# Other places in memory for some weight pieces of a two-layer hybrid network: a second pair in each branch, a cycle of four pairs in one FFN

## The chip, the core and the metric

The kernel runs on one core of a Trainium2 chip. The metric is device time in microseconds of one execution. TensorE (PE in the profile, PEld for its weight loads), VectorE (DVE), ScalarE (ACT), GpSimd (POOL) and SyncE (SP, which issues most DMAs here) run from queues of their own.

## The reference

One sequence of 256 tokens, width 1024, goes through two layers. Each layer has three sub-layers, so there are six branches, which the kernel numbers s = 0 to 5: FFN, hybrid mixer (RG-LRU and SSD), FFN, FFN, mLSTM, FFN. Each branch is normed and modulated by a projection of `c`, and added back through a gate:

```python
def swiglu(h, w_gate, w_up, w_down):
    return (jax.nn.silu(h @ w_gate) * (h @ w_up)) @ w_down
...
h = modulate(x, 0)
x = x + HALF_STEP * (1.0 + mod[:, 0, 2]) * swiglu(h, ffn_w_gate[layer, 0], ffn_w_up[layer, 0], ffn_w_down[layer, 0])
h = modulate(x, 1)
y = hybrid_mixer(h, ...) if layer % 2 == 0 else mlstm_block(h, ...)
x = x + (1.0 + mod[:, 1, 2]) * y
```

D_FF is 2816. All is float32, and every matrix is used once.

## The kernel before, in words

**Weights as a stream.** The host lays all large weight matrices out as 2928 tiles of 128 x 128 in the order of their use, and groups eight of them to a piece: 366 pieces of 128 x 1024 float32, 512 KB each. `Weights._piece` brings one in: a DMA on SP's queue (L90) into one of three `wraw` buffers, a cast on ScalarE to the high part `whi` (L102, fp32r), and a subtraction on VectorE for the low part `wlo` = raw - high (L103). Both parts have six buffers, and a piece is prepared up to four ahead of its use. Between the pieces, `ada_block` (L213 to L220) streams 144 rows of the modulation matrix through the same queue and reduces them on VectorE.

**Matmuls.** The activations stand in memory as high and low parts too, in `hb` (the normed input), `ph` (the FFN's middle) and others. A narrow tile takes three matmuls of 256 columns: high weights with high and with low activations, low weights with high ones (`multiply`, L334 to L336). In the down projections of FFNs and mLSTM a wide tile takes two: high weights with both parts at once, 512 columns (L439), and low weights with 256 (L441). Each matmul loads its 128 x 128 weights first. A narrow piece is thus 24 matmuls, a wide one 16.

**Branches in pieces.** The branches begin at pieces 0, 66, 120, 186, 252 and 300. In an FFN the first 44 pieces (gate and up) are narrow and the last 22 (down) wide; the hybrid branch has 54 narrow pieces; mLSTM has 32 narrow ones and 16 wide. In the last branch the final two pieces count as narrow. I call the branches FFN 0, hybrid, FFN 2, FFN 3, mLSTM and FFN 5. Every branch starts with the norm, whose chain runs through VectorE and ScalarE (`begin`), beside matmuls of 258 columns.

**Places.** Tile pools are laid out one behind the other in each partition. The distance of a part from the start of `hb` is the sum of what lies between: `hb` itself 24576 bytes, a pad of 112 floats (`xpad`, L174), `rs` and two `ssq` tiles of 1024 bytes, three `wraw` of 4096, then six `whi` of 4096 and six `wlo` of 4608. So `whi` begins 24576 + 448 + 3072 + 12288 = 40384 bytes behind `hb`, which is 448 more than a multiple of 512, and the `wlo` tiles likewise. All tiles of a piece lie 512 bytes apart, and all chunks of `hb` 1536, so the remainder by 512 is one number for each part of a piece; I call it the part's place. The high part stands at 448. The low part stands in its tile at an offset of 16 floats, 64 more for odd pieces, 16 more for narrow ones (L93), which gives place 64 (even) or 320 (odd) in narrow pieces and 0 or 256 in wide ones. The moving operands, `ph` and the mLSTM's `yb` among them, stand at place 0.

Of the kernel before, what the change touches and what calls it, by code (L numbers as in the profile page):

```python
# [11 lines left out]
F32 = mybir.dt.float32  # L12
F32R = mybir.dt.float32r
# [6 lines left out]
P = 128  # L20
# [32 lines left out]
SUB_TILES = [FFN_TILES, HYB_TILES, FFN_TILES, FFN_TILES, ML_TILES, FFN_TILES]  # L53
NTILE = sum(SUB_TILES)
PIECE = 8

WIDE = []
for _i, _n in enumerate((ND * NF, 0, ND * NF, ND * NF, ND * 16, ND * NF)):
    _e = sum(SUB_TILES[:_i + 1])
    WIDE.append(((_e - _n) // PIECE, _e // PIECE))  # L60
WIDE[-1] = (WIDE[-1][0], WIDE[-1][1] - 2)
LO_ROW = 384


# [6 lines left out]
class Weights:  # L71
# [14 lines left out]
    def _piece(self, i):  # L86
        nc = self.nc
        w = PIECE * P
        raw = self.raw_pool.tile([P, w], F32, tag="wraw", name=f"wraw{i}")
        nc.sync.dma_start(raw, self.src[i])  # L90


        o = 16 + 64 * (i % 2) + (0 if any(p <= i < q for p, q in WIDE) else 16)  # L93
        hi = self.part_pool.tile([P, w], F32R, tag="whi", name=f"whi{i}")
        lo = self.part_pool.tile([P, w + 128], F32R, tag="wlo", name=f"wlo{i}")[:, o:o + w]
        with self.tc.high_priority(offset=self.ahead):
            if i < 2:
                raw_hi = nc.scalar.copy(hi, raw)
                if i == 1:
                    self.tc.add_manual_dep(raw_hi.ins, self.first[1].ins.name, NOSYNC, reason="the first input first")  # L100
            else:
                raw_hi = nc.scalar.copy(hi, raw)  # L102
            self.last = nc.vector.tensor_tensor(out=lo, in0=raw, in1=hi.bitcast(F32), op=ALU.subtract)  # L103
        if i < 2:
            self.tc.add_manual_dep(self.last.ins, self.first[0].ins.name, NOSYNC, reason="the first input first")
        self.parts[i] = (hi, lo)
        self.splits[i] = (raw_hi, self.last)
        for n, ins in self.after.pop(i, ()):
            self._behind(i, n, ins)
# [25 lines left out]
def body(ctx: ExitStack, tc: tile.TileContext, a, out, dbg=None):  # L135
    nc = tc.nc
# [3 lines left out]
    xp = ctx.enter_context(tc.tile_pool(name="xp", bufs=1))  # L140
# [3 lines left out]
    modp = ctx.enter_context(tc.tile_pool(name="modp", bufs=5))  # L144
    small = ctx.enter_context(tc.tile_pool(name="small", bufs=4))
    tmp = ctx.enter_context(tc.tile_pool(name="tmp", bufs=2))
    ps_mm = ctx.enter_context(tc.tile_pool(name="ps_mm", bufs=4, space=PS))
    ps_ax = ctx.enter_context(tc.tile_pool(name="ps_ax", bufs=1, space=PS))

# [21 lines left out]


    hb = xp.tile([P, ND, 2 * LO_ROW], F32R, name="hb")
    xp.tile([P, 112], F32, name="xpad")  # L174
    hh, hl = hb[:, :, 0:T + 2], hb[:, :, LO_ROW:LO_ROW + T + 2]
    h = [hb[:, k, 0:2 * LO_ROW].rearrange("p (i t) -> p i t", i=2)[:, :, 0:T] for k in range(ND)]
    hx = [(hh[:, k, :], hl[:, k, :]) for k in range(ND)]
# [16 lines left out]
    for b in range(2):  # L194
        q = fpool.tile([P, D], F32, name=f"xsq{b}")
# [893 lines left out]
    w = small.tile([P, 2], F32, tag="rs_w", name="rsw_fin")  # L1089
# [121 lines left out]
```

## Time and profile before

| | |
|---|---|
| median of 3 runs | 1138.76 us (1142.5, 1138.76, 1137.49) |
| the profiled execution's own time | 1143.54 us |
| its span | 1141.8 us |
| TensorE busy | 1116.2 us, 98% of the span |
| weight loads busy | 1064.0 us, 93% |
| VectorE busy | 957.6 us, 84% |
| ScalarE busy | 642.6 us, 56% |
| mean DMA rate | 238 GB/s |

The span is the time from the first to the last profiled instruction. Matmuls overlap in the pipeline, so an engine that is busy all the time can still be working at different paces; the distance between the starts of two matmuls says which. A window's count of instructions includes the two or three that began just before it.

### The profile page before, as it was taken

To read this page: it belongs to the slowest core of one execution; us is meant where nothing else is said; L and a number is where in the kernel's file an instruction comes from. 1 tells how busy PE (TensorE), PEld (TensorE's weight loads), DVE (VectorE), ACT (ScalarE), POOL (GpSimd) and SP (SyncE) were. 2 spreads that over 40 slices of the span, in tenths; PEclk is the share of its full clock that TensorE was granted. 3 is DMA by queue.
4 is the path that set the end of the run, shared out by engine and by line. 5 is a ranking of instruction groups with operands and counts; after the bars stand their busy time and mean duration, and the time that the engine had idled before them with its cause. 6 is when DMAs were issued, how large, how long until landed. Compare 5 with 4: busy or idle time off the path is not lost.

```text
span 1141.8 us, 21905 instructions
## 1 busy us (share of the span) xinstructions
PE 1116.2 (98%) x8548; PEld 1064.0 (93%) x8548; DVE 957.6 (84%) x1831; ACT 642.6 (56%) x1074; POOL 8.7 (1%) x25
## 2 busy tenths in 40 slices
PE   7999999999999999999999998999999999999997
PEld 6999988999988999999899998889999989999987
DVE  7989999999879798788889888989879988766562
ACT  4464444788976554444454454457765556544552
POOL 0000000000000000000000000000000000000000
PEclk8999999999999999999999999999999999999999
DMA  8989989656555658888848899983432364875551
GB/s 332 343 306 360 378 308 323 207 181 193 198 167 170 197 201 316 311 296 306 286 150 291 306 349 328 329 296 109 160 120 93 112 223 149 273 240 201 188 200 41
DMA packets 75273, 272.25 MB, mean 238 GB/s; under 512 B 8449, under 2 KB 9121, under 8 KB 75170
## 3 DMA queue, kind: packets, MB, share of 16 engines
q1 hardware_dynamic: 74160, 268.99, 67.2%
q0 software_dynamic: 432, 1.10, 0.4%
q8 instruction: 67, 1.10, 0.4%
q10 hardware_dynamic: 578, 0.76, 0.2%
q14 instruction: 36, 0.29, 0.1%
HBM read 269.77 MB, written 1.05 MB: 237 GB/s over the span
## 4 chain that ended last, share of the span: by engine, by line
PE 73%; DVE 14%; DMA 6%; ACT 4%; issue 3%; ACTq 0%; SPq 0%
PE od L439 15%; PE gu L335 9%; PE gu L334 9%; PE gu L336 9%; PE od L441 8%; DVE wlo L103 5%; DMA wraw<-in_wst_dram 5%; DVE ada L220 3%; ACT whi L102 2%; DVE hb L351 1%; DMA wgr<-in_ml_wg_dram 1%; PE od L334 1%; PE up L335 1%; PE up L336 1%; DVE ht L348 1%
## 5 line engine op out<-in xcount | busy, mean ns | idle before, releaser
L102 ACT CAST whi<-wraw 128x1024 fp32r<-128x1024 f32 x364 | 380.7, 1049 | 281.3 <-DMA wraw<-in_wst_dram 154.6
L103 DVE TENSOR_TENSOR wlo<-wraw,whi 128x1024 fp32r<-128x1024 f32 x366 | 447.1, 1223 | 94.8 <-ACT whi L102 90.4
L335 PE MATMUL gu<-hb,whi 128*128 128x256 f32 x1312 | 365.8, 280 | 0.1
L336 PE MATMUL gu<-hb,wlo 128*128 128x256 f32 x1312 | 363.0, 278 | 0.0
L334 PE MATMUL gu<-hb,whi 128*128 128x256 f32 x1312 | 360.2, 279 | 1.6 <-ACT hb L350 1.5
L334 PEld LDWEIGHTS gu<-hb,whi 128*128 128x128 f32 x1312 | 245.1, 189 | 2.3 <-ACT hb L350 2.1
L335 PEld LDWEIGHTS gu<-hb,whi 128*128 128x128 f32 x1312 | 246.8, 188 | 0.3 <-DVE hb L351 0.3
L336 PEld LDWEIGHTS gu<-hb,wlo 128*128 128x128 f32 x1312 | 247.1, 188 | 0.0
L439 PE MATMUL od<-ph,whi 128*128 128x512 f32 x682 | 233.9, 391 | 5.7 <-DVE ph L328 5.7
L441 PE MATMUL od<-ph,wlo 128*128 128x256 f32 x682 | 188.9, 277 | 0.0
L220 DVE SCALAR_TENSOR_TENSOR ada<-ada,cact 128x1024 f32<-128x1024 f32 x144 | 175.1, 1219 | 0.0
L439 PEld LDWEIGHTS od<-ph,whi 128*128 128x128 f32 x682 | 128.7, 189 | 33.1 <-DVE ph L328 6.5
L441 PEld LDWEIGHTS od<-ph,wlo 128*128 128x128 f32 x682 | 128.7, 189 | 0.0
L327 ACT CAST ph<-fg 128x256 fp32r<-128x256 f32 x88 | 35.2, 406 | 91.0 <-DVE fg L470 90.6
L446 DVE SCALAR_TENSOR_TENSOR x<-od,gate,x 128x256 f32<-128x256 f32 x87 | 41.6, 482 | 23.0 <-PE od L441 11.9
L328 DVE TENSOR_TENSOR ph<-fg,ph 128x256 fp32r<-128x256 f32 x88 | 36.7, 422 | 12.9 <-ACT ph L327 12.8
L439 PE MATMUL od<-yb,whi 128*128 128x512 f32 x128 | 45.2, 397 | 0.0
L334 PE MATMUL zz<-hb,whi 128*128 128x256 f32 x128 | 37.2, 290 | 0.0
L469 ACT ACTIVATE fg<-gu 128x256 f32<-128x256 f32 x82 | 30.5, 377 | 11.6 <-PE gu L336 11.6
L336 PE MATMUL zz<-hb,wlo 128*128 128x256 f32 x128 | 36.9, 288 | 0.0
L335 PE MATMUL zz<-hb,whi 128*128 128x256 f32 x128 | 36.8, 288 | 0.0
L350 ACT ACTIVATE hb<-ht,shift 128x256 fp32r<-128x256 f32 x48 | 22.6, 505 | 24.2 <-DVE ht L348 24.2
(407 smaller groups left out, 1902.1 us busy)
## 6 DMA issues: line engine op xcount, KB each, us to landing
wraw<-in_wst_dram SPq DMA_DIRECT2D x366, 512.0 KB, 4.3
ada<-in_adaT_dram SPq DMA_DIRECT2D x144, 512.0 KB, 5.4
xn<-in_x_dram SPq DMA_DIRECT2D x2, 512.0 KB, 4.0
wgr<-in_ml_wg_dram POOLq DMA_DIRECT2D x3, 256.0 KB, 5.4
out_dram<-res ACTq DMA_DIRECT2D x2, 128.0 KB, 2.3
out_dram<-res SPq DMA_DIRECT2D x2, 128.0 KB, 2.1
out_dram<-res SPq DMA_DIRECT2D x1, 256.0 KB, 2.5
out_dram<-res ACTq DMA_DIRECT2D x1, 256.0 KB, 2.6
```

Source lines behind the costliest of these rows:

```text
L102: raw_hi = nc.scalar.copy(hi, raw)
L103: self.last = nc.vector.tensor_tensor(out=lo, in0=raw, in1=hi.bitcast(F32), op=ALU.subtract)
L220: nc.vector.scalar_tensor_tensor(out=raw, in0=raw, scalar=1.0, in1=cact, op0=ALU.mult, op1=ALU.mult, accum_out=mods[s][:, m:m + 1])
L327: nc.scalar.copy(hi, src)
L328: nc.vector.tensor_tensor(out=both[:, 1, :], in0=src, in1=hi.bitcast(F32), op=ALU.subtract)
L334: m = nc.tensor.matmul(dst, wh, both[:, 0, :], start=start, stop=False, skip_group_check=True)
L335: nc.tensor.matmul(dst, wh, both[:, 1, :], start=False, stop=False, skip_group_check=True)
L336: nc.tensor.matmul(dst, wl, both[:, 0, :], start=False, stop=stop, skip_group_check=True)
L439: nc.tensor.matmul(bank, wh, both.rearrange("p i t -> p (i t)"), start=(k == 0), stop=False, skip_group_check=True)
L441: nc.tensor.matmul(sums[0], wl, both[:, 0, :], start=False, stop=(k == len(rhs) - 1), skip_group_check=True)
L446: nc.vector.scalar_tensor_tensor(out=xs_t[d], in0=part, scalar=g[:, d:d + 1], in1=xs_t[d], op0=ALU.mult, op1=ALU.add)
L469: nc.scalar.activation(g, b[:, 0:T], AF.Silu)
```

## The change

It gives each piece a pair of places (high, low), written out in a list `PLACES`, where before only the low part's place was set. The `whi` tiles get the same slack of 128 floats as the `wlo` tiles, so that both can be moved. The default pairs stay what they were: (448, 64) and (448, 320) in narrow pieces, (448, 0) and (448, 256) in wide ones. Others get new ones:
- narrow pieces whose number in the branch leaves 6 on division by 11 (6, 17, 28, 39, 50) in all branches but FFN 2: (128, 0)
- wide pieces 1 and 8 of each wide part: (128, 192)
- the 44 narrow pieces of FFN 2: a cycle of (448, 320), (64, 448), (448, 64), (320, 192).

To make room, the pad behind `hb` shrinks from 112 to 16 floats, the scratch for software DMA descriptors at the start of memory from 8192 to 4096 bytes, and a pad of 96 floats ahead of the temporaries brings the pools behind it back to their remainders by 512. With the smaller pad both kinds of tiles begin at place 64, which is why 64 is taken off. The raw pieces, the modulation rows and the small per-column tiles begin 128 bytes further on in a block of 512.

```diff
--- before.py
+++ after.py
@@ -59,6 +59,17 @@
     _e = sum(SUB_TILES[:_i + 1])
     WIDE.append(((_e - _n) // PIECE, _e // PIECE))
 WIDE[-1] = (WIDE[-1][0], WIDE[-1][1] - 2)
+PLACES = []
+for _i in range(NTILE // PIECE):
+    _s = max(s for s in range(6) if sum(SUB_TILES[:s]) // PIECE <= _i)
+    _n = _i - sum(SUB_TILES[:_s]) // PIECE
+    _w = [_i - p for p, q in WIDE if p <= _i < q]
+    if _w:
+        PLACES.append((128, 192) if _w[0] in (1, 8) else (448, 256 * (_i % 2)))
+    elif _s == 2:
+        PLACES.append(((448, 320), (64, 448), (448, 64), (320, 192))[_i % 4])
+    else:
+        PLACES.append((128, 0) if _n % 11 == 6 else (448, 64 + 256 * (_i % 2)))
 LO_ROW = 384
 
 
@@ -90,9 +101,9 @@
         nc.sync.dma_start(raw, self.src[i])
 
 
-        o = 16 + 64 * (i % 2) + (0 if any(p <= i < q for p, q in WIDE) else 16)
-        hi = self.part_pool.tile([P, w], F32R, tag="whi", name=f"whi{i}")
-        lo = self.part_pool.tile([P, w + 128], F32R, tag="wlo", name=f"wlo{i}")[:, o:o + w]
+        oh, ol = ((n - 64) % 512 // 4 for n in PLACES[i])
+        hi = self.part_pool.tile([P, w + 128], F32R, tag="whi", name=f"whi{i}")[:, oh:oh + w]
+        lo = self.part_pool.tile([P, w + 128], F32R, tag="wlo", name=f"wlo{i}")[:, ol:ol + w]
         with self.tc.high_priority(offset=self.ahead):
             if i < 2:
                 raw_hi = nc.scalar.copy(hi, raw)
@@ -144,6 +155,7 @@
     modp = ctx.enter_context(tc.tile_pool(name="modp", bufs=5))
     small = ctx.enter_context(tc.tile_pool(name="small", bufs=4))
     tmp = ctx.enter_context(tc.tile_pool(name="tmp", bufs=2))
+    tmp.tile([P, 96], F32, name="tpad", bufs=1)
     ps_mm = ctx.enter_context(tc.tile_pool(name="ps_mm", bufs=4, space=PS))
     ps_ax = ctx.enter_context(tc.tile_pool(name="ps_ax", bufs=1, space=PS))
 
@@ -171,7 +183,7 @@
 
 
     hb = xp.tile([P, ND, 2 * LO_ROW], F32R, name="hb")
-    xp.tile([P, 112], F32, name="xpad")
+    xp.tile([P, 16], F32, name="xpad")
     hh, hl = hb[:, :, 0:T + 2], hb[:, :, LO_ROW:LO_ROW + T + 2]
     h = [hb[:, k, 0:2 * LO_ROW].rearrange("p (i t) -> p i t", i=2)[:, :, 0:T] for k in range(ND)]
     hx = [(hh[:, k, :], hl[:, k, :]) for k in range(ND)]
@@ -1200,7 +1212,7 @@
     from concourse.bass_utils import run_bass_kernel_spmd
 
     arrays = layouts(inputs)
-    nc = bacc.Bacc("TRN2", target_bir_lowering=False, num_devices=1, dynamic_dma_scratch_size=8192)
+    nc = bacc.Bacc("TRN2", target_bir_lowering=False, num_devices=1, dynamic_dma_scratch_size=4096)
     args = {n: nc.dram_tensor(f"in_{n}_dram", v.shape, mybir.dt.from_np(v.dtype), kind="ExternalInput").ap()
             for n, v in arrays.items()}
     out = nc.dram_tensor("out_0_dram", (T, D), F32, kind="ExternalOutput").ap()
```

## Rows read from the trace of the kernel before

**Rows 1.** The page: the group of instructions that makes the low parts.
```profile
L103 DVE TENSOR_TENSOR wlo<-wraw,whi 128x1024 fp32r<-128x1024 f32 x366 | 447.1, 1223 | 94.8 <-ACT whi L102 90.4
```

**Rows 2.** Busy by stretch: PE, PEld, DVE, ACT, POOL (count); clock, DMA share, GB/s.
```profile
61.50:141.40 79.90, 79.90 (x675) 79.90 (x674) 73.88 (x118) 40.71 (x63) 0.00 (x0) 1.00 0.94 351
279.90:296.90 17.00, 17.00 (x145) 17.00 (x144) 16.32 (x29) 14.83 (x29) 0.00 (x0) 1.00 0.70 230
412.20:521.10 108.90, 108.90 (x919) 108.90 (x918) 89.64 (x131) 54.12 (x81) 0.00 (x0) 1.00 0.85 300
593.80:702.60 108.80, 108.80 (x962) 108.80 (x961) 96.97 (x160) 52.80 (x79) 1.08 (x2) 1.00 0.86 304
964.30:1073.10 108.80, 108.80 (x962) 108.80 (x961) 77.64 (x112) 57.66 (x87) 0.00 (x0) 1.00 0.66 223
```

**Rows 3.** Timeline of PE, narrow: piece 127 to 164, then piece 191 to 230, first matmuls.
```profile
415.51 0.28 PE L334 MATMUL gu<-hb,whi 128*128 128x256 f32 x1
...
521.08 0.40 PE L439 MATMUL od<-ph,whi 128*128 128x512 f32 x1
...
596.54 0.28 PE L334 MATMUL gu<-hb,whi 128*128 128x256 f32 x1
...
702.62 0.39 PE L439 MATMUL od<-ph,whi 128*128 128x512 f32 x1
```

**Rows 4.** Timeline of PE, wide: piece 166 to 185, then piece 289 to 299, first matmuls.
```profile
526.55 0.39 PE L439 MATMUL od<-ph,whi 128*128 128x512 f32 x1
...
578.23 0.39 PE L439 MATMUL od<-ph,whi 128*128 128x512 f32 x1
...
920.67 0.40 PE L439 MATMUL od<-yb,whi 128*128 128x512 f32 x1
...
948.67 0.40 PE L439 MATMUL od<-yb,whi 128*128 128x512 f32 x1
```

**Rows 5.** Timeline of PE first wide piece of FFN 0 (44) and the next.
```profile
141.38 0.39 PE L439 MATMUL od<-ph,whi 128*128 128x512 f32 x1
...
144.11 0.39 PE L439 MATMUL od<-ph,whi 128*128 128x512 f32 x1
```

**Rows 6.** Timeline of PE around a wait of FFN 0.
```profile
55.47 1.07 PE L334 MATMUL gu<-hb,whi 128*128 128x256 f32 x5
56.37 0.28 PE L335 MATMUL gu<-hb,whi 128*128 128x256 f32 x1
...
56.97 0.28 PE L335 MATMUL gu<-hb,whi 128*128 128x256 f32 x1
```

**Rows 7.** The chain that ended last, shares: FFN 2 narrow, mLSTM wide.
```profile
by line: PE gu L335 34.1%; PE gu L334 33.2%; PE gu L336 32.8%
...
by line: PE od L439 64.2%; PE od L441 32.2%; PE hT L1024 3.3%; PE zz L334 0.3%; PE zz L336 0.3%; PE zz L335 0.3%
```

**Rows 8.** The chain, in order of time: end of FFN 0, hybrid branch.
```profile
193.95 0.49 DVE x L446
...
209.12 5.58 DMA wraw<-in_wst_dram
...
258.90 4.33 DMA wraw<-in_wst_dram
```

**Rows 9.** The chain, in order of time: a row of FFN 3.
```profile
605.43 5.28 DMA wraw<-in_wst_dram
```

**Rows 10.** Waits (us, times, longest): 141 to 196, 521 to 581, 596 to 720 us.
```profile
DVE x L446 <- PE od L441: 1.4, 2, 1.2
...
ACT whi L102 <- PE od L439: 24.7, 18, 1.7
...
PE od L439 <- DVE ph L328: 5.7, 2, 3.3
```

**Rows 11.** Timeline of FFN 0: the split of piece 54, its first matmul.
```profile
164.95 1.22 DVE L103 TENSOR_TENSOR wlo<-wraw,whi 128x1024 fp32r<-128x1024 f32 x1
...
168.59 0.39 PE L439 MATMUL od<-ph,whi 128*128 128x512 f32 x1
```

## What I expect, written before the run

> **What bounds the kernel now.** Read first the busy times by stretch [rows 2]. [...] So there are two paces, and the clock is not what tells them apart. The timeline gives them exactly [rows 3]: pieces 127 to 163 of FFN 2 are 37 x 24 = 888 matmuls of 256 columns in 521.08 - 415.51 = 105.57 us, 118.9 ns each; pieces 191 to 229 of FFN 3 are 936 in 106.08 us, 113.3 ns each. Shapes, places in memory and engines are the same. A wide tile (512 and 256 columns) has two paces too [rows 4]: 51.68 us / 152 = 340.0 ns in FFN 2, 28.00 us / 80 = 350.0 ns in the mLSTM branch. I call them the quick and the slow pace. The slow one costs 24 x 5.55 ns = 0.133 us a narrow piece and 8 x 10 ns = 0.080 us a wide one.
>
> Next, where the pace changes. In FFN 0 PE waits between 55.47 and 56.37 us (five matmuls that take 0.90 us instead of 0.57), and from there to 56.97 us five starts lie 120 ns apart [rows 6]; the whole rest of the narrow part stays slow (675 in 79.9 us, [rows 2]). At 141.38 us the shape changes to wide, and the first wide piece takes 144.11 - 141.38 = 2.73 us, the quick 8 x 340 ns but for 0.01 [rows 5]. So a pace, once taken, holds for tens of microseconds; a wait can turn it to slow, and another pattern of reads, without any wait, has turned it back.
>
> Then the chain that ended last, for where a slow pace counts at all. In FFN 2 it is matmuls alone, and in the wide part of the mLSTM branch 96% matmuls of its two lines [rows 7]: a nanosecond there is a nanosecond of the end. Behind FFN 0 the chain goes over to VectorE at 193.95 us and through the transfer of raw weights at 209.12 and 258.90 us [rows 8]. In FFN 3 it runs over transfers and splits, as in the row at 605.43 us [rows 9], and PE idles there once for 5.7 us behind the last ph [rows 10]. In those places PE's pace is covered.
>
> **The change part by part.** No instruction, transfer or wait is added, taken away or moved: 63 of 366 pieces get their high and low parts at another distance from the moving operand, and the pools around them shift. What is priced is therefore the pace alone.
>
> Narrow pieces with number 6, 17, 28, 39 (and 50) of each branch but FFN 2 now stand at (128, 0), in all 20; wide pieces 1 and 8 at (128, 192), in all 10. I take them as resets: for one piece (24 or 16 matmuls) the two streams of reads that PE makes meet at other places, and the pace is taken anew. No row shows these pairs. Below, a reset does nothing to the pace and costs nothing; above, it turns a slow stretch quick. I take the second, since the only change of pattern without a wait that the rows show did that [rows 5]. The FFN 2 cycle moves 33 of its 44 narrow pieces, two of every four with the high part at another place; by the same reading it never stays slow.
>
> What that gives, in the profiled execution:
> - FFN 2: the 37 slow pieces, 37 x 0.133 = 4.9 us. Nothing else is near: VectorE is busy 89.6 of 108.9 us [rows 2], and in the wide part behind it ScalarE waits 24.7 us for PE to free a buffer [rows 10], so the splits can catch up what they lose. Late next is FFN 3's norm, which starts that much earlier too. I take 4.9.
> - FFN 0: the reset at piece 17 frees pieces 18 to 43, 26 x 0.133 = 3.5 us, but not all of it arrives. VectorE is busy 73.9 of 79.9 us [rows 2], and the split of piece 54 ends at 166.17 us, 2.4 us ahead of its first matmul at 168.59 [rows 11]: no more than 2.4 can pass there. VectorE itself waits for PE only 1.4 us before the seam [rows 10], and the chain goes on through VectorE [rows 8]. So between 0 and 2.4; I take 1.4.
> - Hybrid: the same slow pace (145 starts in 17.0 us, [rows 2], as against about 152 at the quick one). The resets at pieces 83 and 116 would free about 14 pieces, 1.9 us, half of it behind ScalarE and transfers [rows 8]: 0.9, between 0 and 1.9.
> - mLSTM wide: pieces 286 to 299 behind the reset at 285, 14 x 0.080 = 1.1 us on the chain [rows 7].
> - FFN 3 narrow: quick already, and PE has 5.7 us of idle time there [rows 10]: 0 either way.
> Sum 8.3 us.
>
> Against it stands what a reset costs where the stream was quick. Priced from below at nothing and from above at the slow pace: four narrow ones of FFN 5 and five wide ones on the chain (two each in FFN 2 and FFN 5, one behind FFN 3's wait), 4 x 0.133 + 5 x 0.080 = 0.9 us; those of FFN 0 and FFN 3's narrow part lie under the covers named above. I take 0.5.
>
> The raw weights and the streamed modulation rows now begin 128 bytes further in a block of 512. All 366 splits read from the old place, 1223 ns each [rows 1], so no row shows the other. A split slower or faster by 1% would be 12 ns a piece, under VectorE's 19 us of idle time in FFN 2 [rows 2]; only FFN 0's margin would feel it, 66 x 12 ns = 0.8 us. I take 0. The smaller descriptor scratch serves only the eight transfers that GpSimd issues, most of them for FFN 3; I price it at 0, and if one came late, PE's 5.7 us of idle time in FFN 3 [rows 10] would grow by as much.
>
> Sum: 8.3 - 0.5 = 7.8 us, bounds 10.3 (all of FFN 0 and hybrid, no cost) and 4.0 (FFN 2's 4.9 alone, less 0.9).
>
> The profiled execution took 1143.54 us, 4.8 above the median of 1138.76. From its own time the sum gives 1143.54 - 7.8 = 1135.7. If the timed runs hold the same slow stretches and the difference is the profiler's, the median falls to 1131.0. The timed runs themselves spread over 5.0 us, which is what FFN 2's stretch alone is worth, so I think some of them had it quick; but nothing proves it. I forecast 1133, between the two, 0.5% below the median, which is the edge of what I call a change: 0.5% is 5.7 us, so faster means below 1133.1 and slower above 1144.5.
>
> [...]
>
> **The rivals.**
> - The place doesn't decide. The pace would then be taken at the waits [rows 6] and kept through every reset. For it: both paces occur at the same pairs [rows 3]. Against it: the turn at 141.38 us without a wait [rows 5]. Time: that of before, 1138.8, with its spread of 1137.5 to 1142.5. Chance 0.13.
> - Half works: the resets do, the FFN 2 cycle does not (it keeps default pairs in two of four pieces, so it may be slow in those), or the other way round. Without FFN 2's 4.9 us there are left 2.9 us: 1138.8 - 2.9 = 1135.9; with the cycle alone and the other parts at their cost, 4.9 - 0.9 = 4.0: 1134.8 from the median, up to 1139.5 from the profiled time. About 1137. Chance 0.13.
> - The resets throw quick stretches into the slow pace (the other side). Then FFN 5 from piece 307 on loses 37 x 0.133 = 4.9 us, and the wide parts of FFN 2 (20 pieces), FFN 3 behind the wait (14) and FFN 5 (19) lose 53 x 0.080 = 4.2 us; FFN 3's narrow part stays covered. With FFN 2 no better, 1138.8 + 9.1 = 1147.9. It is slower by my bound from 5.7 us of these on, that is FFN 5's narrow part and ten wide pieces, if FFN 2's gain is gone too; with that gain it is 1143. Against it: a new pattern led to the quick pace [rows 5]. Chance 0.12, three quarters of it slower.
>
> **How the numbers follow.** My forecast has 0.62: between 1128.5 (10.3 below the median) and 1136.5, with a little over half of it below 1133.1. That makes 0.35 faster, and 0.27 within 0.5%; "half works" adds 0.02 to faster and 0.11 to same, "place doesn't decide" 0.13 to same, "resets harm" 0.03 to same and 0.09 to slower. Faster 0.37, same 0.54, slower 0.09; since the hybrid and mLSTM branches have many short slow spells (as in [rows 2]) that I counted only in part, I move 0.04 from same to faster. The range leaves out the harm above 1141 and the lowest tail: 1129 to 1141.
>
> **What would show it.** FFN 2 at about 940 to 960 starts in 108.8 us instead of 919; FFN 0 behind piece 17 at 113.3 ns; wide tiles of the mLSTM branch at 340 ns from piece 286 on; reset pieces themselves of at most 2.85 us. The chain of FFN 0's end starts on VectorE earlier than 193.95 us by 1 to 2. The forecast is wrong if FFN 2 stays at 118.9, if FFN 3 or FFN 5 fall to it behind a reset, or if PE begins to wait for splits in FFN 0 by more than it gained.

## The result and the profile after

The changed kernel takes 1136.97 us (median of 20 runs, 1129.76 to 1143.28) where the kernel before takes 1142.09 beside it (20 runs, 1136.58 to 1148.23): a ratio of 0.9948, 95% interval 0.9928 to 0.9968. That is 0.52% less, just past the 0.5% that I called a change (the interval reaches to both sides of it), and 4 us above my forecast of 1133. Of the three runs of before that I had seen (median 1138.76), two lay at the lower end of its spread. The profiled execution took 1137.13 us as against 1143.54.

Busy by stretch after, in the columns of [rows 2]: FFN 0 from piece 18 to 43, FFN 2 from piece 127 to 163, FFN 5 from piece 306 on.

```profile
67.90:138.90 71.00, 71.00 (x627) 71.00 (x626) 67.44 (x110) 36.40 (x55) 0.00 (x0) 1.00 0.96 357
411.20:511.90 100.70, 100.70 (x891) 100.70 (x890) 83.39 (x121) 49.66 (x74) 0.00 (x0) 1.00 0.87 313
962.80:1047.80 85.00, 85.00 (x750) 85.00 (x749) 60.60 (x84) 43.29 (x66) 0.00 (x0) 1.00 0.69 236
```

FFN 2's 37 pieces, 888 matmuls, now take 100.7 us, 113.4 ns each; before it was 105.57 [rows 3]. FFN 0's 26 pieces, 624 matmuls in 71.0 us, stand at the quick pace but for the two reset pieces among them. FFN 5 is quick as before; its row holds 750 starts with three reset pieces in it, and 752 or 753 in the kernels below that have none there.

Timeline of PE after: first matmul of the reset piece 17 and of piece 18, then of the wide pieces 289 and 299 of the mLSTM branch.

```profile
65.16 0.28 PE L346 MATMUL gu<-hb,whi 128*128 128x256 f32 x1
...
68.00 0.28 PE L346 MATMUL gu<-hb,whi 128*128 128x256 f32 x1
...
914.49 0.39 PE L451 MATMUL od<-yb,whi 128*128 128x512 f32 x1
...
941.74 0.39 PE L451 MATMUL od<-yb,whi 128*128 128x512 f32 x1
```

The reset piece takes 2.84 us, 0.12 more than a quick one and within 0.02 of a piece at the slow pace (24 x 118.9 ns = 2.85 us). The wide pieces take 27.25 us, 340.6 ns a tile, as against 28.00 us before [rows 4].

By branch, from the timeline's first matmul of each (us). For each matmul that reads a weight piece, the distance to the next start is compared with the quick pace: "pace" adds up the excesses under 20 ns, "waits" those of 20 ns or more.

| branch | length before, after | difference | pace before, after | waits before, after |
|---|---|---|---|---|
| before piece 0 | 14.6, 15.4 | +0.9 | | |
| FFN 0 | 187.0, 183.8 | -3.2 | 4.4, 1.2 | 2.7, 2.8 |
| hybrid | 188.7, 187.1 | -1.6 | 5.2, 4.3 | 12.7, 11.8 |
| FFN 2 | 191.0, 186.0 | -5.1 | 5.8, 0.8 | 1.2, 1.3 |
| FFN 3 | 189.4, 192.0 | +2.6 | 0.6, 1.5 | 8.1, 9.8 |
| mLSTM | 181.1, 180.5 | -0.7 | 3.0, 1.9 | 10.6, 11.1 |
| FFN 5 to the end | 190.0, 190.6 | +0.6 | 0.7, 1.3 | 0.3, 0.3 |

Each entry is rounded by itself; unrounded, the differences add up to -6.4 us, that of the two spans (1141.8 and 1135.4). At FFN 0's end the chain that ended last, which left the matmuls only at 193.95 us before [rows 8], now runs over splits and transfers long ahead of it:

```profile
152.41 6.22 DMA wraw<-in_wst_dram
...
161.07 6.26 DMA wraw<-in_wst_dram
...
194.05 5.82 DMA wraw<-in_wst_dram
```

FFN 3 gave 2.6 back. Its rows after, where piece 232 waits for the last ph, in the columns of [rows 2]; then the two of before that answer to the last two (piece 232 begins at 699.64 after and at 708.06 before); then the wait that answers to [rows 10]:

```profile
700.00:704.00 4.00, 1.34 (x9) 0.95 (x8) 3.27 (x6) 2.67 (x5) 0.00 (x0) 0.97 1.01 368
704.00:708.00 4.00, 0.90 (x3) 0.39 (x3) 4.00 (x7) 2.25 (x4) 0.00 (x0) 0.50 0.89 280
708.00:712.00 4.00, 4.00 (x13) 3.42 (x14) 2.65 (x4) 1.29 (x2) 0.00 (x0) 0.50 0.95 349
712.00:716.00 4.00, 4.00 (x19) 3.45 (x19) 3.82 (x6) 0.94 (x2) 0.00 (x0) 0.75 0.95 365
```

```profile
716.40:720.40 4.00, 4.00 (x17) 3.45 (x17) 2.77 (x4) 1.67 (x2) 0.00 (x0) 0.66 0.97 369
720.40:724.40 4.00, 4.00 (x25) 3.53 (x25) 3.47 (x6) 0.93 (x3) 0.00 (x0) 1.00 1.01 394
```

```profile
PE od L451 <- DVE ph L340: 5.8, 2, 3.1
```

The wait itself is as long as before (5.8 us, 5.7 in [rows 10]). What grew is what follows it: PE idles, the granted clock falls to 0.50, and it stays low longer than before (a mean of 0.50 and then 0.75 in the last two rows, 0.66 and 1.00 before), and 4 us hold 13 and then 19 matmuls where they held 17 and 25. The DMA share is 0.89 or more throughout, and of the chain from 585 to 730 us 32.1% is transfers of raw weights, its costliest line: the branch is bound by its weights, as [rows 9] said.

### The profile page after: what moved, and what is told of

It is laid out like the page before. It is cut to its first block, busy times and chain, and to the rows that moved or that the text cites. A ratio compares the mean times of both kernels' runs of the same rounds, so it can differ in the third digit from the quotient of the medians.

```text
span 1135.4 us, 21905 instructions
## 1 busy us (share of the span) xinstructions
PE 1109.3 (98%) x8548; PEld 1057.5 (93%) x8548; DVE 955.4 (84%) x1831; ACT 642.0 (57%) x1074; POOL 8.8 (1%) x25
## 4 chain that ended last, share of the span: by engine, by line
PE 61%; DVE 18%; DMA 13%; ACT 5%; issue 3%; ACTq 0%; SPq 0%; DVEq 0%
PE od L451 12%; DMA wraw<-in_wst_dram 11%; DVE wlo L114 7%; PE gu L346 7%; PE gu L347 7%; PE gu L348 7%; PE od L453 6%; DVE ada L232 3%; ACT whi L113 3%; DVE hb L363 1%; DMA wgr<-in_ml_wg_dram 1%; DVE ht L360 1%; PE od L346 1%; PE up L347 1%; PE up L348 1%
## 5 line engine op out<-in xcount | busy, mean ns | idle before, releaser
L114 DVE TENSOR_TENSOR wlo<-wraw,whi 128x1024 fp32r<-128x1024 f32 x366 | 446.1, 1221 | 97.1 <-ACT whi L113 95.1
L458 DVE SCALAR_TENSOR_TENSOR x<-od,gate,x 128x256 f32<-128x256 f32 x87 | 41.5, 480 | 20.1 <-PE od L348 9.7
L453 PE MATMUL od<-yb,wlo 128*128 128x256 f32 x128 | 35.5, 279 | 0.0
```

The source lines that it names most:

```text
L453: nc.tensor.matmul(sums[0], wl, both[:, 0, :], start=False, stop=(k == len(rhs) - 1), skip_group_check=True)
L458: nc.vector.scalar_tensor_tensor(out=xs_t[d], in0=part, scalar=g[:, d:d + 1], in1=xs_t[d], op0=ALU.mult, op1=ALU.add)
```

## The experiments

All are edits of the list of pairs in the changed kernel; shifted pools, slack and scratch stay. Ratios are to the kernel before, run beside each. In the fences "85 us" is a stretch of a narrow part from its ninth piece (FFN 2: 128) or seventh (FFN 3: 192, FFN 5: 306): at the quick pace it holds 750 starts and the two or three that began before it, at the slow one 715 and those.

**Default pairs everywhere.**

```diff
-        PLACES.append((128, 192) if _w[0] in (1, 8) else (448, 256 * (_i % 2)))
-    elif _s == 2:
-        PLACES.append(((448, 320), (64, 448), (448, 64), (320, 192))[_i % 4])
+        PLACES.append((448, 256 * (_i % 2)))
     else:
-        PLACES.append((128, 0) if _n % 11 == 6 else (448, 64 + 256 * (_i % 2)))
+        PLACES.append((448, 64 + 256 * (_i % 2)))
```

> Every piece at the default pair of the kernel before; only the pools are shifted (raw weights and modulation rows 128 bytes further in a block of 512, smaller descriptor scratch, slack in the high parts). If the places decide the pace (theory), FFN 2's narrow part and the end of the mLSTM branch can run slow as before (118.9 and 350 ns) and the time is that of the kernel before: ratio 0.998 to 1.002. If the shifted pools or the chance of a wait gave the gain (rival), the ratio is that of the changed kernel, 0.995, with FFN 2 at 113.3 ns.

Ratio 0.9995 (0.9974 to 1.0017). Busy by stretch: FFN 0 from piece 18, FFN 2.

```profile
67.30:132.30 65.00, 65.00 (x576) 65.00 (x575) 61.36 (x98) 33.50 (x51) 0.00 (x0) 1.00 0.97 355
414.60:499.60 85.00, 85.00 (x718) 85.00 (x717) 69.29 (x101) 41.63 (x62) 0.00 (x0) 1.00 0.90 312
```

FFN 2 is slow again, so the shifted pools are not what made it quick. But FFN 0 is quick without any reset: at the default pairs both paces occur, and which one comes is not settled by the pairs.

**The cycle alone, and the resets alone.** Each is the changed kernel with the other edit taken back to the default pairs.

> The cycle of four pairs in FFN 2 alone, every other piece at its default pair. Theory: FFN 2's 37 slow pieces become quick, 4.9 us less than the kernel before (ratio 0.9957), and FFN 0, the hybrid and the mLSTM branch keep their slow stretches. Rival (places do not matter): ratio 1.000 and FFN 2 slow or quick by chance. If the resets were only a cost, this is the faster version: 0.993 or less.

> The resets alone, FFN 2's narrow part at the default pairs. Theory: FFN 2 slow again if a slow stretch starts there (loses 4.9 us of the changed kernel's gain), the others as in the changed kernel: ratio 0.998 to 1.001, since the gain of FFN 0 and the hybrid branch (about 4 us) was spent in FFN 3 and FFN 5 (3.1 us). If the resets carry the gain, 0.995.

Cycle alone: 0.9972 (0.9944 to 1.0000), median 1137.35. Resets alone: 0.9986 (0.9959 to 1.0014), median 1140.71. Busy by stretch, the cycle alone: FFN 2, then FFN 3 from piece 212 to 228.

```profile
413.70:498.70 85.00, 85.00 (x752) 85.00 (x751) 71.58 (x106) 43.27 (x65) 0.00 (x0) 1.00 0.91 320
644.40:692.40 48.00, 48.00 (x406) 48.00 (x405) 42.97 (x69) 22.87 (x34) 0.00 (x0) 1.00 0.93 338
```

FFN 2 is quick with the cycle. FFN 3, at default pairs, turned slow at a gap of 0.1 us in piece 211 and stayed so to the end of its narrow part, 406 starts in 48 us (quick would be 424 and the two or three before); behind the wait at piece 232 the wide pieces 234 to 251 were slow as well. Yet this branch, 191.6 us, was no longer than in the changed kernel (192.0), since the wait at piece 232 fell to 5.3 us with what follows it, from 7.7: pace in FFN 3 is covered, as two kernels below show more plainly.

Busy by stretch, the resets alone: FFN 2, then the hybrid branch from piece 89 on.

```profile
415.60:500.60 85.00, 85.00 (x752) 85.00 (x751) 69.99 (x104) 42.43 (x63) 0.00 (x0) 1.00 0.89 312
277.40:291.40 14.00, 14.00 (x121) 14.00 (x120) 12.96 (x24) 11.98 (x24) 0.00 (x0) 1.00 0.71 232
```

Here FFN 2 came out quick at its default pairs; I had expected it slow. And the hybrid branch stays slow from piece 78 to 97, right through the reset pieces 83 and 94, and again from 104 to 111 around 105 (121 starts where the quick pace gives 126, below). Of these only 94 is a plain test: gaps of 0.5 and 0.4 us lie at the end of 83, and a wait of 1.3 us right behind 105, and a pace can turn slow at a wait, as FFN 0's did at 55.47 us in before [rows 6].

Other narrow resets stood in slow stretches with no wait behind them, and there the quick pace followed at once. Behind piece 280 of the mLSTM branch, pieces 281 and 282: before, changed kernel, resets alone. Then piece 270: the resets alone, with the reset at 269, and the default pairs everywhere.

```profile
895.40:900.80 5.40, 5.40 (x47) 5.40 (x47) 4.41 (x13) 3.31 (x5) 0.00 (x0) 1.00 0.79 261
889.15:894.55 5.40, 5.40 (x50) 5.40 (x49) 4.39 (x13) 2.94 (x5) 0.00 (x0) 1.00 0.86 273
888.15:893.55 5.40, 5.40 (x50) 5.40 (x49) 4.54 (x13) 3.06 (x5) 0.00 (x0) 1.00 0.83 247
...
840.70:843.40 2.70, 2.70 (x27) 2.70 (x25) 2.27 (x9) 1.33 (x2) 0.00 (x0) 1.00 0.52 184
845.30:848.00 2.70, 2.70 (x25) 2.70 (x24) 2.28 (x8) 1.33 (x2) 0.00 (x0) 1.00 0.51 171
```

The same holds behind piece 116 of the hybrid branch, in both kernels with resets.

**One pair for a whole part.** These tell whether a pair has a pace of its own.

```diff
+        PLACES.append({0: (64, 448), 2: (128, 0), 3: (448, 320), 5: (320, 192)}[_s])
```

(in the four FFNs; the wide pieces of FFN 0 and mLSTM at (128, 192)), and

```diff
+        PLACES.append({0: (448, 64), 2: (448, 0), 3: (480, 352), 5: (384, 64)}[_s])
```

> One pair for a whole narrow part: (64, 448) in FFN 0, (128, 0) in FFN 2, (448, 320) in FFN 3, (320, 192) in FFN 5; the wide pieces of FFN 0 and mLSTM all at (128, 192). If the pace belongs to the pair, FFN 2 runs at 118.2 ns throughout (44 pieces at 0.116 us, 5.1 us more than quick), the wide parts of FFN 0 and mLSTM at 346 ns (0.050 us a piece), and the other three narrow parts at 113.3 ns whenever no wait has turned them. If it is the change of pair that costs, only the first piece of each part is slow.

> One pair for a whole narrow part: (448, 64) in FFN 0, (448, 0) in FFN 2, (480, 352) in FFN 3, (384, 64) in FFN 5. The pairs that ran quick have both parts at 64 beyond a multiple of 128, the pair (128, 0) has both at a multiple of 128. If the remainder of the high part by 128 decides, FFN 5 (384) is slow in two of three matmuls (about 116.5 ns) and FFN 2 in one of three (about 115 ns); FFN 0 at 113.3; FFN 3 in between. If only the pace at the last wait counts, each part is at 113.3 or 118.9 throughout, whatever its pair.

Busy by stretch, first kernel: FFN 0 from piece 18, FFN 2, FFN 5, then 30 us of mLSTM's wide part from piece 288.

```profile
67.10:132.10 65.00, 65.00 (x576) 65.00 (x575) 61.81 (x98) 34.71 (x54) 0.00 (x0) 1.00 0.96 356
415.50:500.50 85.00, 85.00 (x721) 85.00 (x720) 68.83 (x101) 41.35 (x62) 0.00 (x0) 1.00 0.89 310
966.40:1051.40 85.00, 85.00 (x753) 85.00 (x752) 60.91 (x85) 43.73 (x67) 0.00 (x0) 1.00 0.72 236
914.70:944.70 30.00, 30.00 (x175) 26.47 (x174) 25.45 (x39) 18.76 (x27) 0.00 (x0) 1.00 0.77 241
```

Second kernel: FFN 0, FFN 2, FFN 3, FFN 5.

```profile
68.20:133.20 65.00, 65.00 (x549) 65.00 (x548) 62.46 (x99) 34.78 (x53) 0.00 (x0) 1.00 0.97 360
423.30:508.30 85.00, 85.00 (x724) 85.00 (x723) 70.25 (x102) 41.55 (x63) 0.00 (x0) 1.00 0.90 314
605.10:690.10 85.00, 85.00 (x717) 85.00 (x716) 75.50 (x121) 39.59 (x59) 1.07 (x2) 1.00 0.89 313
974.50:1059.50 85.00, 85.00 (x724) 85.00 (x723) 59.06 (x82) 41.52 (x64) 0.00 (x0) 1.00 0.70 230
```

In these parts the pace goes with the pair. The reset pair (128, 0) is slow by itself: 721 starts, 85 / 718.5 = 118.3 ns, in all 37 pieces from 127 on with no wait among them. So are (448, 0) and (384, 64) (117.8 ns) and (480, 352) (119.0 ns). (64, 448) and (320, 192) ran quick (576 starts in 65 us, 753 in 85 us), and so did (448, 320) in FFN 3 (752 in 85 us). The default place (448, 64), held without alternating, was slow in FFN 0 (549 starts in 65 us) from a wait in piece 14 on, as the default pairs were in before, and quick in pieces 2 to 13. The wide reset pair is slow by itself too: 175 starts where the changed kernel has 179 in the same 30 us. My split by thirds (only the matmuls with the moved part slow) did not hold: (448, 0) and (384, 64) came out alike. Each of these two kernels was run once, in 1140.15 and 1152.51 us.

The second kernel also shows that pace in FFN 3 is covered. There this branch ran at the slow pace from its fifth piece to its end and took 188.5 us; with every piece at the reset pairs (next) it took 188.6. In the twelve other kernels it took 188.4 to 192.0. In the two slow ones its waits shrink to 0.3 and 1.2 us (6.3 to 9.8 in the others), and in the second kernel the clock does not fall, over 10 us from piece 232 on (the changed kernel's mean clock over the same 10 us is 0.71).

```profile
719.15:729.15 10.00, 10.00 (x59) 8.77 (x58) 8.10 (x13) 4.36 (x7) 0.00 (x0) 1.00 0.96 344
```

**Every piece at the reset pairs**, which makes the suspected cost large: (128, 0) in all narrow pieces, (128, 192) in all wide ones.

> Every narrow piece at (128, 0), every wide one at (128, 192): nothing changes from piece to piece. If these pairs are slow by themselves, FFN 2 and FFN 5 lose 5.1 us each against quick, their wide parts and mLSTM's 2.8 us, FFN 0 up to 5: 13 to 18 us above the changed kernel, ratio to before 1.006 to 1.012. If only a change of pair costs, the time is that of the changed kernel or less: 0.993 to 0.996.

Ratio 1.0104 (1.0057 to 1.0151), median 1154.05 beside 1142.98. FFN 5 has 721 starts in the 85 us and FFN 2 the same:

```profile
972.90:1057.90 85.00, 85.00 (x721) 85.00 (x720) 58.88 (x82) 41.48 (x63) 0.00 (x0) 1.00 0.70 229
```

Place alone, with the same instructions, moves this kernel by 11 us in this direction.

**The cycle in all narrow parts**, without the (128, 0) pieces.

> The cycle of four pairs in the narrow parts of all branches, no (128, 0) piece; the wide pieces as in the changed kernel. Theory: every narrow part runs at 113.3 ns, so the hybrid branch loses its two slow stretches that the (128, 0) pieces did not end (about 2 us less) and FFN 5 its four pieces of 0.116 us (0.5 us): 1 to 2.5 us below the changed kernel, ratio to before 0.9925 to 0.994. If the cycle holds the quick pace only where it was quick anyway, the ratio is 0.995 to 1.000 and slow stretches appear in FFN 0 or in the hybrid branch.

Ratio 0.9955 (0.9934 to 0.9975). The pace did what was expected: its excess over quick is 7.5 us in the whole execution (10.9 in the changed kernel, 19.7 in before), and outside the branches' starts no slow stretch of a narrow part is longer than 30 matmuls (a piece has 24). The time did not follow. The hybrid branch took 190.3 us, longer than before (188.7). Busy by stretch around its piece 112, changed kernel first, then this one:

```profile
363.00:368.00 5.00, 4.37 (x35) 3.96 (x34) 4.35 (x10) 1.66 (x3) 0.00 (x0) 1.00 0.72 233
368.00:373.00 5.00, 4.28 (x36) 3.99 (x35) 3.76 (x7) 2.97 (x5) 0.00 (x0) 1.00 0.64 233
```

```profile
363.00:368.00 5.00, 2.23 (x20) 2.04 (x18) 2.86 (x6) 0.78 (x1) 0.00 (x0) 0.94 0.81 237
368.00:373.00 5.00, 4.37 (x19) 4.20 (x20) 3.86 (x8) 2.14 (x5) 0.00 (x0) 0.50 0.36 124
```

and there, in this kernel (its lines stand two lower), the wait and then the chain:

```profile
PE od L344 <- ACT ylb L337: 3.4, 1, 3.4
```

```profile
360.97 6.15 DMA wraw<-in_wst_dram
367.22 1.04 ACT whi L111
368.27 0.31 ACT ylb L337
```

PE reaches the projection sooner, waits 3.4 us (1.3 in the changed kernel) for ScalarE's ylb, which stands in its queue behind a cast whose raw weights land after 6.15 us (4.30 in the changed kernel), and the granted clock falls to 0.50 behind the wait. In this execution the quicker pace is spent there, and more than it.

**A cycle for the wide pieces too**, by analogy: (448, 256), (64, 384), (448, 0), (320, 128).

> The cycle of four pairs in all narrow parts and a cycle of (448, 256), (64, 384), (448, 0), (320, 128) in all wide parts; no (128, 0) and no (128, 192). If the slow stretches go where the pair of places changes from piece to piece among pairs that are quick by themselves, no stretch of slow pieces is longer than two outside the branches' starts, and the wide resets' 10 x 0.05 us go too: 0.5 to 1.5 us below the changed kernel, ratio 0.993 to 0.996. If the gain of the pace is given back in the waits for weights, the ratio stays at 0.9955 and the waits of the hybrid branch and FFN 3 grow.

Ratio 0.9997 (0.9976 to 1.0019). Neither expectation: the narrow parts are quick, but every wide piece at (64, 384) or (320, 128) is slow. FFN 2 from piece 166 on, 291 starts where the changed kernel has 296 in 50 us:

```profile
520.80:570.80 50.00, 50.00 (x291) 44.07 (x290) 42.21 (x63) 24.99 (x33) 1.06 (x2) 1.00 0.87 300
```

High parts at 64 and 320 ran quick under 256 moving columns (with low parts at 448 and 192, 113.3 ns) and slow under 512 (with low parts at 384 and 128).

**One pair of the cycle for all narrow pieces**, and the default pairs once more (the first and the last with the wide cycle).

> All narrow pieces at one pair of the cycle, (64, 448); wide pieces in the wide cycle. If the pair by itself cannot stay slow, the hybrid branch has no slow stretch behind its waits (pieces 78 to 95 and 105 to 111 at 113.3 ns) and FFN 2 is quick. If it is the change from piece to piece that ends a slow stretch, some stretch of ten or more pieces at 118.9 ns stands behind a wait, most likely in the hybrid branch.

> All narrow pieces at another pair of the cycle, (320, 192); wide pieces at their default pairs. The same two expectations as for the pair (64, 448); one of the two pairs may be immune and the other not.

> All narrow pieces at their default pairs, wide pieces in the wide cycle. If slow stretches belong to the default pairs and start at waits, the hybrid branch has one of ten or more pieces from 78 to 97 and FFN 2 one from piece 127 to 163, in more than half of such executions; the wide parts have none. If FFN 2 is quick, its slow stretch is a matter of chance, as in the kernel with resets alone.

Each was run once. Outside the branches' starts both single pairs (1137.73 and 1138.99 us) have no slow stretch longer than one piece in any narrow part, the hybrid branch included. With the default pairs FFN 0 and FFN 2 are slow from piece 14 and 125 to the end of their narrow parts, and the execution took 1149.16 us; the hybrid branch, against expectation, was quick from piece 88. The hybrid branch from piece 89 at (64, 448), then FFN 2 at the default pairs:

```profile
277.40:291.40 14.00, 14.00 (x126) 14.00 (x126) 13.58 (x26) 12.61 (x25) 0.00 (x0) 1.00 0.76 241
```

```profile
419.80:504.80 85.00, 85.00 (x717) 85.00 (x716) 67.89 (x100) 40.34 (x61) 0.00 (x0) 1.00 0.88 305
```

So no change from piece to piece is needed; one such pair is enough. Both parts stand elsewhere in these pairs, and no run tells whether the high part's place alone would do.

**A candidate**: (64, 448) in all narrow pieces, the wide ones as in the changed kernel.

> All narrow pieces at the one pair (64, 448), which showed no slow stretch; wide pieces as in the changed kernel, with the pair (128, 192) in pieces 1 and 8. Theory: no slow stretch in any narrow part, no piece at 0.116 us, wide parts at 340 ns behind piece 8 at the latest. Against the changed kernel that is worth 0.5 us in FFN 5 and the harm of chance stretches in FFN 0: ratio 0.993 to 0.9955. If the hybrid branch's pace, now quick throughout, comes back as a longer wait at pieces 112 to 114 with the clock falling there, up to 3 us are lost: 0.996 to 0.998.

Ratio 0.9952 (0.9922 to 0.9983), median 1137.07: no better than the changed kernel. Its pace excess is the lowest of all, 6.4 us, its waits are 41.5 us (37.1 in the changed kernel), 16.7 of them in the hybrid branch. Around piece 112:

```profile
363.00:368.00 5.00, 1.54 (x9) 1.17 (x8) 2.26 (x5) 2.32 (x4) 0.00 (x0) 0.77 0.68 213
368.00:373.00 5.00, 5.00 (x27) 5.00 (x27) 2.93 (x6) 0.66 (x3) 0.00 (x0) 0.55 0.48 137
```

No version here is shown to beat the changed kernel. How much of the pace turns into waits differs from one execution to another. Of the five kernels whose hybrid branch was quick but for single pieces, four took 189.6 to 191.0 us there; the fifth, at (64, 448) with the wide cycle, took 187.2, as long as the changed kernel. Of the nine others eight took 187.1 to 189.2 us, and one 192.7.

## Why the prediction was right or wrong

**FFN 2: right, 4.9 us predicted, 5.1 measured.** That pairs like those of the cycle keep a narrow part quick is shown by count over these 14 kernels, one profiled execution of each. Narrow FFN parts at the default pairs without resets were slow for ten pieces or more in 6 of 16. Those with the high part at 64 or 320 in at least every second piece were so in none of 24, and none had a slow stretch longer than 30 matmuls behind the branch's first four pieces. It is not a gain of 4.9 us in every run, however: at its default pairs FFN 2 was slow in three of four profiles, and quick in the kernel with the resets alone.

**The rival that places don't decide fell.** It would have given 0; the runs differ, with 113.3 against 118.3 ns by place alone, held through whole parts, and 11 us over the kernel. They show that the place of the weights sets the pace, not by what. The moving operands stood at place 0 in every run.

**The resets: right more often than not, and dearer than nothing.** I read a reset as a piece that makes the stream take its pace anew. Narrow ones in a slow stretch, with no wait behind them, turned it quick in five of six cases: behind 116 and 280 in the changed kernel and with the resets alone, and behind 269 with the resets alone; not behind 94 there. At the same places, kernels that were slow at default pairs stayed slow in twelve of twelve. The wide reset at piece 8 did it too: FFN 3 was quick behind piece 238 in the changed kernel (2.72 us a piece, 2.80 in 234 to 237) and in the candidate, while slow wide parts at default pairs stayed slow to their end in before (mLSTM, 2.80 us a piece), in the kernel with the cycle alone (FFN 3 from 234), in the second kernel of single pairs (FFN 2, with 288 starts in 50 us from piece 166 on, and FFN 3) and in the one at (320, 192) (FFN 2). It isn't the only way out: in the mLSTM branch piece 285 was slow and 286 turned quick without a reset, with default pairs everywhere and with the cycle alone. The reset's pair has a slow pace of its own (118.3 ns), which is what a reset costs. As for the rival that resets do harm, 24 narrow resets in quick stretches left them quick; but behind piece 6 of FFN 0 about one piece was slow in both kernels, and just ahead of the wait behind 105 both were slow where the six kernels at default pairs were quick. What failed is the step from the resets to the gain: as the next three paragraphs say, little of what I put down to them in FFN 0, the hybrid branch and the mLSTM branch is shown to be theirs.

**FFN 0: 1.4 predicted, 3.2 measured, for another reason.** It was quick before the reset at 17 came, and quick without resets in two of the four profiles that have default pairs there. So its gain is the luck of this execution. My cap held no better: the split of piece 54 starts at 163.02 us in place of 164.95 [rows 11], so it moved along with PE.

**Hybrid: 0.9 predicted, 1.6 measured,** by half in pace (the slow stretch went on through reset 83, with 2.85 us in piece 87, and ended at the wait of piece 88, with 2.72 us in 89; the reset at 116 freed only the last pieces) and by half in shorter waits.

**mLSTM: 1.1 predicted, 0.7 measured.** The wide pieces gained 27.25 for 28.00 us as expected; 0.5 us more went into waits. But with default wide pairs they were quick from piece 288 on at the latest in four of five profiles (179 starts in 30 us), and slow in before alone, so this gain is not shown to be the reset's either.

**FFN 3: 0 predicted, 2.6 given back.** That pace is covered there was right, as the two kernels with FFN 3 at the slow pace showed. What I priced at nothing is the time behind the wait: more of it passed at a granted clock of 0.50 (piece 233 took 4.62 us, 1.4 more than before), and pieces 234 to 237 were slow (2.80 us each, 2.72 before). Whether the change caused this is open: with the same resets in FFN 3, the kernel with the resets alone took 189.3 us there, and the profiles spread from 188.4 to 192.0. In this trace PE idled for VectorE's last ph, whose chain goes back to a transfer of 5.81 us at 693.74, and came back at 0.50, with 13 matmuls in 4.00 us.

**The reset's cost: 0.5 predicted, 0.66 by its terms** (four narrow pieces of FFN 5 at 0.116 us, four wide ones of FFN 2 and FFN 5 at 0.050): nearer the upper bound than the lower (0.116 for 0.133, 0.050 for 0.080). FFN 5 grew by 0.6. The shifted raw weights cost nothing: a split takes 1221 ns after, 1223 before [rows 1].

**The level.** Against the sum of 7.8 us stand 6.4 in the profiled executions and 5.1 in the medians. Had I known the median of 20 runs, the same sum would have given 1134.3. That the time fell inside my range is in part luck: 3.2 us in FFN 0 and 2.6 us the other way in FFN 3, neither of them for a reason that I gave. Of my cases "half works", with 1137, came nearest in time. In kind it isn't the case: the cycle does what it says, and the resets mostly do. Whether the resets add anything in the timed runs isn't settled: the intervals of the cycle alone, the resets alone and both overlap.

## What to carry to other kernels

When one stretch of identical matmuls shows two distances between starts at one granted clock (113.3 and 118.9 ns at 1.00 here), try the place of the weights in memory: hold one pair of places through a whole stage, look at its pace in one profile, and only then mix pairs. Test each shape by itself: (448, 0), slow when held through a narrow part (117.8 ns), is one of the two default pairs of wide parts that ran quick (340.0 ns a tile in FFN 2 [rows 4]). Before counting a quicker pace as time, ask what PE meets next. With the cycle in all narrow parts it met a transfer of 6.15 us in the hybrid branch: the wait there grew from 1.3 to 3.4 us, and the granted clock behind it was 0.50 where it had been 1.00.

## What the runs showed of the hardware that was not expected

- Three kinds of pair, narrow: always quick in these runs (113.3 ns; (64, 448), (320, 192)), always slow (117.8 to 119.0 ns; (128, 0), and (448, 0), (384, 64) and (480, 352) in one part each), and one that can be either and holds it for tens of pieces (113.3 or 118.9 ns; high part at 448, low at 64 and 320). The quick ones and the last all have both parts 64 beyond a multiple of 128, but so much alone does not tell the last from the first.
- One piece at a pair that is itself slow can end a slow stretch of the pieces behind it: five of six cases without a wait, against none of twelve at default pairs.
- A slow pace can outlive the part that it began in: in the second kernel of single pairs the wide pieces of FFN 2 at default pairs were slow to their end behind a narrow part at (448, 0), 288 starts in 50 us, while behind (128, 0) in the first they were quick, 297 starts. Why, and why the default pairs have two paces, stays open; no run here looked at single reads.
